# Two-token one-hots, groups built on a budget, and gate loads placed behind weight loads in a PEER layer

## The chip, the cores and the metric

The kernel runs on one core of one Trainium2 chip. The metric is the device time of one execution in microseconds. A core has five engines with instruction streams of their own: PE (TensorE, matrix multiplies; the loads of its stationary operand are listed as PEld), DVE (VectorE), ACT (ScalarE), POOL (GpSimd) and SP (SyncE, which here only issues DMAs). A wait on another engine or on a DMA stops everything that stands behind it in the same stream.

## The reference

Two layers of one transformer block and then two layers of a second block are applied to 256 tokens of width 1024, in float32. The change touches the feed-forward part of the second block alone, which chooses 128 of 16384 experts for each token (8 heads, 16 choices each):

```python
def peer_ffn(xn, wq, sub_keys, u_tab, v_tab):          # t = 256 tokens, d = 1024
    q = jnp.matmul(xt, wq).reshape(t, PEER_HEADS, 2, PEER_SUBDIM)
    scores = jnp.einsum('thcd,hcnd->thcn', q, sub_keys)
    sv, si = lax.top_k(scores, PEER_TOPK)              # 16 of 128, on either half
    cand_s = (sv[:, :, 0, :, None] + sv[:, :, 1, None, :]).reshape(t, PEER_HEADS, -1)
    cand_i = (si[:, :, 0, :, None] * 128 + si[:, :, 1, None, :]).reshape(t, PEER_HEADS, -1)
    best_s, best_p = lax.top_k(cand_s, PEER_TOPK)
    idx = jnp.take_along_axis(cand_i, best_p, axis=-1) # expert = 128 i + j
    gate = jax.nn.softmax(best_s, axis=-1)
    act = jnp.einsum('td,thkd->thk', xt, u_tab[idx])
    wgt = jax.nn.gelu(act) * gate
    return jnp.einsum('thk,thkd->td', wgt, v_tab[idx])
```

## The kernel before

`peer` does not gather rows of the tables. It computes the activations of all 16384 experts for all 256 tokens, multiplies them by a dense table of gates that is zero where an expert was not chosen, and multiplies the product by the whole table V. Each layer therefore streams both tables through the core in units of 128 x 1024 float32 (512 KB): 128 units of U, then 128 of V.

A unit is fetched by SP into `wx` (3 buffers; the next fetch is queued when a buffer is free), copied in reduced precision by ACT to `wh` and its remainder formed by DVE in `wl` (4 buffers each, lines 118 and 121 of `split`). PE then makes three products of every pair, high by high, high by low and low by high.

**U.** 64 steps in two halves of 32. A step (`u_step`) takes two units, runs 48 matmuls of 256 columns into the accumulator `pj`, and ACT applies Gelu from `pj` into `at0` (first half) or `at1` (second half). Meanwhile the first half carries the choice of the experts. Its gates reach the product in two ways. For tokens 0 to 127 POOL scatters them into a table in DRAM, `gates` (`scatter_gates`, which runs far into the second half). For tokens 128 to 255 they are built on the chip, four tokens at a time, in 32 groups: `build(g)` lets DVE form one-hots of the two halves of the expert number (`oi`, `oj`, 512 elements on each partition), multiply `oj` by the gate in three bf16 parts (`og`, 1536 elements), then PE multiplies them (12 matmuls of 128 x 128 into `ps`, three for each token), and DVE multiplies `at0` and the finished part of `at1` by `ps`; where `at1` is not yet computed ACT copies `ps` into it, and a later `u_step` multiplies its Gelu (in the tile `y`) onto that. Four tokens are interleaved, so that one token's one-hot has elements four apart:

```python
io = self.t(ip, [128, 128, 4], BF16, tag="io")
self.mm(ps[:, k], oi[:, :, k], og[:, n, :, k], k == 0 and n == 0, n == 2)
```

Before, one group is built behind each of the 32 steps of U's second half.

**V.** 64 steps. `v_split` loads two planes of the table for the tokens 0 to 127 (`gate`, 128 KB, 3 buffers), multiplies the activations by them on DVE (`at<-at,gate`), and splits the product into `eh` (ACT) and `el` (DVE). `v_step` runs 24 matmuls of 512 columns of its two units against it, accumulated in four banks (`big`). The split for step n+1 is issued in step n. A scheduler of the framework puts the instructions of each engine in an order by priorities and estimated times; loads that need no buffer yet in use may be queued early.

Of the kernel before, what the change touches and what calls it, by code (L numbers as in the profile page):

```python
# [12 lines left out]
BF16 = mybir.dt.bfloat16  # L13
# [3 lines left out]
AF = mybir.ActivationFunctionType  # L17
OP = mybir.AluOpType
AX = mybir.AxisListType

T = 256
# [32 lines left out]
EARLY = 1  # L54
WARM = 10
LAG, TAIL, AHEAD, HOLD = 4, 2, 2, (2, 6)
SIDE_Q, SIDE_S = 2500, 2800
UQ_SIZES = [768, 512]
S2_SIZES = [1024] * 26

# [1 line left out]
class Net:  # L62
# [83 lines left out]
    def weights(self, ap, sizes, per=1024, beside=iter(())):  # L146
        k, off = 0, 0
        while k < len(sizes):
            n, tot = 0, 0
            while k + n < len(sizes) and tot + sizes[k + n] <= per:  # L150
                tot += sizes[k + n]
                n += 1
            x = self.t(self.wp, [128, per], tag="wx", bufs=WX)
            self.nc.sync.dma_start(x[:, :tot], ap[:, off:off + tot])
            next(beside, None)
            at = 0
            for s in sizes[k:k + n]:
# [61 lines left out]

    def load_gates(self, l, n, pool):  # L220

        g = self.t(pool, [128, 2, 128], tag="gate", bufs=3)
        d = self.nc.sync.dma_start(g, self.gates[l][:, 2 * n:2 * n + 2]).ins
        for b in self.landed:
            self.tc.add_manual_dep(d, b.name, SYNC, reason="the gates have landed")
        return g
# [809 lines left out]
    def peer(self, l):  # L1036
# [3 lines left out]
        with ExitStack() as ctx:  # L1040
            ip = ctx.enter_context(self.pool("pi"))
            idx = self.t(ip, [128, 128], U32, tag="idx")
            gs = [self.t(ip, [128, 8, 16], tag=f"gs{tt}") for tt in range(2)]
# [13 lines left out]
            def u_step(at, jp, tb=0):  # L1057
# [4 lines left out]
                a = at[:, 2 * jp:2 * jp + 2]  # L1062
                self.act(a[:, :, :T - tb], ps[:, :, :T - tb], AF.Gelu_apprx_tanh)
# [5 lines left out]
            def build(g):  # L1069


                t0, done = 124 - 4 * g, 2 * g + 2
                oi, oj = (self.t(self.op, [128, 128, 4], BF16, tag=n, bufs=2) for n in ("oi", "oj"))
                og = self.t(self.op, [128, 3, 128, 4], BF16, tag="og", bufs=2)
                self.tt(oi, io, iT[:, None, t0:t0 + 4].to_broadcast([128, 128, 4]), OP.is_equal)
                self.tt(oj, io, jT[:, None, t0:t0 + 4].to_broadcast([128, 128, 4]), OP.is_equal)
                self.tt(og, oj[:, None].to_broadcast([128, 3, 128, 4]),
                        gT[:, :, None, t0:t0 + 4].to_broadcast([128, 3, 128, 4]), OP.mult)
                yield 1900
                ps = self.ps([128, 4, 128])  # L1080
                for k in range(4):
                    for n in range(3):
                        self.mm(ps[:, k], oi[:, :, k], og[:, n, :, k], k == 0 and n == 0, n == 2)
                ps = ps.rearrange("p t j -> p j t")
                t0 += 128
                a0, a1 = at0[:, :, t0:t0 + 4], at1[:, :, t0:t0 + 4]
                self.tt(a0, a0, ps[:, :64], OP.mult)
                self.tt(a1[:, :done], a1[:, :done], ps[:, 64:64 + done], OP.mult)
                if done < 64:
                    self.copy(a1[:, done:], ps[:, 64 + done:])  # L1090
                yield 700

            parts, loaded = {}, {}

            def g_load(n):
                if n < 64:
                    loaded[n] = self.load_gates(l, n, early)
# [11 lines left out]
            def first_split():  # L1109
                for n in range(2):  # L1110
                    g_load(n)
                v_split(0, early)

            def v_step(at, jp, half):
                units = [(next(w), x) for x in parts.pop(32 * half + jp)]
# [24 lines left out]
            with self.pool("pn") as npool:  # L1140
                lead = self.enter(npool, "add", self.v("n2"), w, self.t(npool, [128, 8, T], tag="xnew"))
                self.dump(f"xc{l}", self.xT)
                if l < DEPTH - 1:
                    nc.sync.dma_start(keep, self.xT)
                self.hctx.close()
                self.xctx.close()
                self.open_xs()
                pool = sctx.enter_context(self.pool("pk", "right"))
                self.token_column()
                if l == DEPTH - 1:  # L1150
                    nc.sync.dma_start(keep, self.rows_of(npool))
# [5 lines left out]
                self.copy(io, it[:, :, None].to_broadcast([128, 128, 4]))  # L1157
# [12 lines left out]
            self.hctx.close()  # L1170
            self.open_xt()
            if l < DEPTH - 1:
# [5 lines left out]
                end = to_output  # L1178
            vctx = ExitStack()
            vp = vctx.enter_context(self.pool("pv", "right"))  # L1180
            for half, at in enumerate((at0, at1)):
                weave(lambda jp: v_step(at, jp, half), iter(()), 0)
            vctx.close()
# [3 lines left out]
    def select(self, l, pool, w, lead, normed, io16, gs, idx, turned):  # L1187
# [63 lines left out]
        def rest_of_ranks():  # L1251
            yield from normed
            pend.sort(key=lambda x: x[0])
            for tt in range(2):
# [5 lines left out]
                for r in range(8):  # L1260
                    n = 16 if r == 0 else 8
                    o = 0 if r == 0 else 8 + 8 * r
# [5 lines left out]
                    yield 760  # L1268

                bt = best[tt]  # L1270
                g = gs[tt]
# [9 lines left out]
                pf = self.t(pool, [128, 128], tag="pf", bufs=2)  # L1281
# [37 lines left out]
                iT, jT, gT = turned  # L1319
                ps = self.ps([128, 3, 128])  # L1320
# [217 lines left out]
```

## Time and profile before

| | before |
|---|---|
| median of 3 runs | 2614.23 us (2613.8 to 2616.39) |
| profiled execution, and its span | 2614.9 us, 2613.0 us |
| granted TensorE clock | 0.996 of full speed |
| PE busy | 2560.8 us (98%) |
| PEld busy | 2366.2 us (91%) |
| DVE busy | 1835.9 us (70%) |
| ACT busy | 1383.7 us (53%) |
| POOL busy | 463.4 us (18%) |
| HBM | 179 GB/s over the span |

The span is what the trace covers; the execution's own time has 1.9 us around it. Busy time of PE is not time at its peak: matmuls are pipelined, and a matmul's listed duration is longer than the spacing of two in a row. In layer 1 U's second half runs from about 1046 to 1276 us and V to 1641 us; in layer 2 V begins at 2250 us and ends at 2608 us.

### The profile page before, as it was taken

What the parts mean: (1) busy time and instruction counts of PE and PEld (TensorE: products, weight loads), DVE (VectorE), ACT (ScalarE), POOL (GpSimd) and SP (SyncE); (2) the same over time, 40 slices, a digit from 0 to 9 for tenths busy, and PEclk for the clock granted to TensorE, in tenths of its full rate; (3) what the DMA queues carried; (4) which work ended last, traced back from release to release, by engine and by line L of the source; (5) the groups of instructions that cost most, each with busy time, mean ns of one, the idle gap of its engine ahead of it and who ended that gap; (6) DMA issues with size and microseconds to landing.
All of it is one profiled execution on the core that took longest, in us unless ns stands there. A gap on an engine that the chain in (4) does not pass through costs nothing.

```text
span 2613.0 us, 46153 instructions
## 1 busy us (share of the span) xinstructions
PE 2560.8 (98%) x18042; PEld 2366.2 (91%) x18042; DVE 1835.9 (70%) x3511; ACT 1383.7 (53%) x2128; POOL 463.4 (18%) x261
## 2 busy tenths in 40 slices
PE   8999999999999999999999999999999999999999
PEld 7799997999999999999878888999999999878887
DVE  6688777877887995666665555877994666675555
ACT  6565566655676554444444444776554443344443
POOL 0000000000000077773000000000178772000000
PEclk9999999999999999999999999999999999999999
DMA  8756652566535576665576666635576665676664
GB/s 281 235 179 192 183 174 79 153 192 183 175 116 185 170 185 186 149 150 149 193 249 203 194 194 193 185 107 187 173 191 179 148 150 148 212 248 194 194 194 158
DMA packets 195098, 470.95 MB, mean 180 GB/s; under 512 B 54644, under 2 KB 89588, under 8 KB 193856
## 3 DMA queue, kind: packets, MB, share of 16 engines
q1 hardware_dynamic: 158016, 467.86, 56.9%
q0 software_dynamic: 36864, 0.15, 3.6%
q8 instruction: 141, 2.31, 0.3%
q14 instruction: 77, 0.63, 0.1%
HBM read 447.86 MB, written 20.05 MB: 179 GB/s over the span
## 4 chain that ended last, share of the span: by engine, by line
PE 85%; DMA 6%; DVE 6%; ACT 2%; issue 1%; SPq 0%; ACTq 0%; DVEq 0%
PE pj L132 46%; PE big L132 31%; PE ps L132 7%; DMA gate<-gates 4%; DVE wl L121 2%; DMA wx<-in_w 1%; ACT wh L118 1%; PE ps L573 1%; DVE el L121 1%; DVE xn L124 0%; DVE at L121 0%; DVE xT L121 0%; DMA wx<-in_wq 0%; DVE xl L124 0%; DVE c L124 0%
## 5 line engine op out<-in xcount | busy, mean ns | idle before, releaser
L118 ACT ACTIVATE wh<-wx 128x1024 fp32r<-128x1024 f32 (+1 forms) x800 | 844.4, 1057 | 898.7 <-PE pj L132 356.1
L121 DVE TENSOR_TENSOR wl<-wx,wh 128x1024 fp32r<-128x1024 f32 (+1 forms) x800 | 975.0, 1220 | 453.8 <-ACT wh L118 446.4
L132 PE MATMUL pj<-xh,wh 128*128 128x256 f32 x3136 | 897.3, 286 | 10.5 <-ACT wh L118 7.9
L132 PE MATMUL pj<-xl,wh 128*128 128x256 f32 x3136 | 889.6, 284 | 3.3 <-DVE xl L124 2.7
L132 PE MATMUL pj<-xh,wl 128*128 128x256 f32 x3136 | 889.1, 284 | 3.8 <-DVE wl L121 3.8
L209 POOL DMA_INDIRECT gates<-gs,idx x256 | 462.9, 1808 | 1712.6 <-DVE idx L129 1591.8
L132 PEld LDWEIGHTS pj<-xh,wh 128*128 128x128 f32 x3136 | 601.2, 192 | 12.8 <-ACT wh L118 8.3
L132 PEld LDWEIGHTS pj<-xl,wh 128*128 128x128 f32 x3136 | 600.5, 191 | 7.9 <-DVE xl L124 6.5
L132 PEld LDWEIGHTS pj<-xh,wl 128*128 128x128 f32 x3136 | 599.9, 191 | 6.6 <-DVE wl L121 5.7
L132 PE MATMUL big<-wh,el 128*128 128x512 f32 x1024 | 402.1, 393 | 10.4 <-DVE el L121 10.3
L132 PE MATMUL big<-wh,eh 128*128 128x512 f32 x1024 | 400.0, 391 | 11.6 <-ACT eh L118 11.6
L132 PE MATMUL big<-wl,eh 128*128 128x512 f32 x1024 | 399.9, 390 | 0.0
L132 PEld LDWEIGHTS big<-wh,el 128*128 128x128 f32 x1024 | 193.1, 189 | 58.4 <-DVE el L121 19.2
L132 PEld LDWEIGHTS big<-wh,eh 128*128 128x128 f32 x1024 | 193.0, 189 | 52.6 <-ACT eh L118 12.2
L132 PEld LDWEIGHTS big<-wl,eh 128*128 128x128 f32 x1024 | 193.1, 189 | 39.6
L121 DVE TENSOR_TENSOR at<-at,ps 128x256 f32<-128x256 f32 (+20 forms) x128 | 45.1, 352 | 131.6 <-PE ps L132 131.6
L132 PE MATMUL ps<-og,oi 128*128 128x128 bf16 x768 | 101.5, 297 | 0.0
L132 PE MATMUL big<-gh,wh 128*128 128x256 f32 x352 | 99.1, 282 | 0.0
L132 PE MATMUL big<-gl,wh 128*128 128x256 f32 x352 | 98.9, 281 | 0.0
L132 PE MATMUL big<-gh,wl 128*128 128x256 f32 x352 | 98.8, 281 | 0.0
L121 DVE TENSOR_TENSOR at<-at,gate 128x256 f32<-128x256 f32 x128 | 52.9, 422 | 58.4 <-DMA gate<-gates 58.0
L121 DVE TENSOR_TENSOR el<-at,eh 128x512 fp32r<-128x512 f32 x128 | 87.2, 684 | 0.0
(355 smaller groups left out, 3309.0 us busy)
## 6 DMA issues: line engine op xcount, KB each, us to landing
wx<-in_u SPq DMA_DIRECT2D x256, 512.0 KB
wx<-in_v SPq DMA_DIRECT2D x256, 512.0 KB
wx<-in_wm SPq DMA_DIRECT2D x132, 512.0 KB
wx<-in_w SPq DMA_DIRECT2D x88, 512.0 KB
gates<-zero SPq DMA_DIRECT2D x128, 128.0 KB
wx<-in_wo SPq DMA_DIRECT2D x32, 512.0 KB
wx<-in_wq SPq DMA_DIRECT2D x32, 512.0 KB
gate<-gates SPq DMA_DIRECT2D x128, 128.0 KB
```

The lines of the kernel that those rows point to most:

```text
L118: return self.nc.scalar.activation(out, in_, AF.Copy)
L121: return self.nc.vector.tensor_tensor(out, a, b, op=op)
L132: return self.nc.tensor.matmul(ps, w, x, start=start, stop=stop, skip_group_check=True)
L209: d = self.nc.gpsimd.indirect_dma_start(flat, IndirectOffsetOnAxis(ap=idx[:, p:p + 1], axis=0), g[:, p:p + 1], None, compute_op=OP.add).ins
L573: self.nc.tensor.transpose(tp[:, kt, qt * 128:(qt + 1) * 128], p[:, qt, kt * 128:(kt + 1) * 128], self.ident)
```

## The change

It has four parts.

1. One-hots interleave two tokens instead of four (`io` is 128 x 2, `oi` and `oj` are 2 x 128 x 2). `oi` and `oj` stay one operation each; `og` becomes two operations of 768 elements. The 12 matmuls of a group stay, and read elements two apart.
2. The groups are a generator, `builds`, woven into U's second half on a budget: each of the 32 steps adds 3100, a group costs 2000 for its one-hots and matmuls and 750 for what uses `ps`. So a group's `ps` is used a step after it was started, now and then two groups fall into one step, and all are done some three steps before U's end. The tile `y` goes: Gelu is taken in place in `pj`, and DVE multiplies from there.
3. The first gates and V's first split (`first_split`) are issued in the last of U's steps, from a tile of their own; only steps 1 and 2 have their gates loaded at V's start.
4. `load_gates` makes each load of gates stand behind the latest unit's fetch in SP's queue (`self._dep(d, self.fetched)`).

```diff
-            x = self.t(self.wp, [128, per], tag="wx", bufs=WX)
-            self.nc.sync.dma_start(x[:, :tot], ap[:, off:off + tot])
+            self.fetched = self.nc.sync.dma_start(x[:, :tot], ap[:, off:off + tot]).ins
...
-        g = self.t(pool, [128, 2, 128], tag="gate", bufs=3)
+        g = pool if n == 0 else self.t(pool, [128, 2, 128], tag="gate", bufs=3)
         d = self.nc.sync.dma_start(g, self.gates[l][:, 2 * n:2 * n + 2]).ins
+        self._dep(d, self.fetched)
...
-            io = self.t(ip, [128, 128, 4], BF16, tag="io")
+            io = self.t(ip, [128, 128, 2], BF16, tag="io")
+            first = self.t(ip, [128, 2, 128], tag="gate")
+            built = [0]
...
-                if tb:
-                    y = self.t(self.op, [128, 2, 128], tag="y", bufs=2)[:, :, :tb]
-                    self.act(y, ps[:, :, T - tb:], AF.Gelu_apprx_tanh)
-                    self.tt(a[:, :, T - tb:], a[:, :, T - tb:], y, OP.mult)
+                if built[0]:
+                    self.act(ps[:, :, n:], ps[:, :, n:], AF.Gelu_apprx_tanh)
+                    self.tt(a[:, :, n:], a[:, :, n:], ps[:, :, n:], OP.mult)
...
+            def builds(pairs):
+                for t0 in range(124, -1, -4):
+                    oi, oj = (self.t(self.op, [128, 2, 128, 2], BF16, tag=n, bufs=b) for n, b in (("oi", 2), ("oj", 1)))
...
+                    ps = self.ps([128, 4, 128])
+                    for a in range(2):
+                        og = self.t(self.op, [128, 3, 128, 2], BF16, tag="og", bufs=3)
...
+                                self.mm(ps[:, 2 * a + k], oi[:, a, :, k], og[:, n, :, k], a == 0 and k == 0 and n == 0,
+                                        n == 2)
+                    yield 2000
...
+                    built[0] += 4
+                    yield 750
...
             def v_split(n, pool):
                 if n < 64:
-                    g_load(n + 2)
+                    if n:
+                        g_load(n + 2)
...
             with self.pool("po") as self.op:
-                for g in range(32):
-                    u_step(at1, g, 4 * g)
-                    for _ in build(g):
-                        pass
-            early = ctx.enter_context(self.pool("pf"))
-            first_split()
+                weave(u_second, builds(pairs), SIDE_G, first_split)
```

How the order of instructions moves is seen at three places. In the rows, `x<-y,z` is what is written and read, and the number is the tile's.

On DVE, in a step late in U's second half of layer 1, before:

```order
L121 TENSOR_TENSOR oj_15377<-io_9886,jT_9884 128x512
L121 TENSOR_TENSOR wl_15170<-wx_15166,wh_15169 128x1024
L121 TENSOR_TENSOR at_10626<-at_10626,ps_15119 128x64x4
L121 TENSOR_TENSOR wl_15227<-wx_15224,wh_15226 128x1024
L121 TENSOR_TENSOR at_13122<-at_13122,y_15110 128x2x88
L121 TENSOR_TENSOR at_13122<-at_13122,ps_15119 128x46x4
L121 TENSOR_TENSOR oi_15288<-io_9886,iT_9883 128x512
L121 TENSOR_TENSOR og_15290<-oj_15289,gT_9885 128x1536
L121 TENSOR_TENSOR oj_15464<-io_9886,jT_9884 128x512
```

And in the same place after the change:

```order
L121 TENSOR_TENSOR oi_15589<-io_9885,iT_9882 128x512
L121 TENSOR_TENSOR oj_15590<-io_9885,jT_9883 128x512
L121 TENSOR_TENSOR og_15594<-oj_15590,gT_9884 128x768
L121 TENSOR_TENSOR og_15602<-oj_15590,gT_9884 128x768
L121 TENSOR_TENSOR at_10626<-at_10626,ps_15505 128x64x4
L121 TENSOR_TENSOR at_13123<-at_13123,ps_15416 128x52x4
L121 TENSOR_TENSOR at_13123<-at_13123,pj_15433 128x2x112
L121 TENSOR_TENSOR wl_15614<-wx_15611,wh_15613 128x1024
L121 TENSOR_TENSOR wl_15645<-wx_15641,wh_15644 128x1024
```

Before, the products of `at0` and `at1` with `ps` (15119) stood around one `wl` and the product with `y`. After, they stand behind the next group's one-hots and both operations on `og`; the product of `at1` reads the `ps` of the group before (15416) the one that the product of `at0` reads (15505), and both `wl` of the step's units follow.

On SP, at the turn from U to V in layer 1 (`in_v` are V's units, `keep` the residual, `xT` its place in the memory that U's inputs leave), before:

```order
L154 DMA wx_16033<-in_v 128x1024
L1173 DMA xT_15941<-keep_9889 128x2048
L223 DMA gate_15926<-gates_95 128x256
L223 DMA gate_15928<-gates_95 128x256
L223 DMA gate_15930<-gates_95 128x256
L154 DMA wx_16039<-in_v 128x1024
L223 DMA gate_15970<-gates_95 128x256
L223 DMA gate_16014<-gates_95 128x256
L223 DMA gate_16057<-gates_95 128x256
L223 DMA gate_16101<-gates_95 128x256
L223 DMA gate_16144<-gates_95 128x256
L223 DMA gate_16188<-gates_95 128x256
```

And after:

```order
L154 DMA wx_16067<-in_v 128x1024
L1180 DMA xT_15971<-keep_9889 128x2048
L223 DMA gate_15976<-gates_95 128x256
L223 DMA gate_15978<-gates_95 128x256
L223 DMA gate_16004<-gates_95 128x256
L154 DMA wx_16073<-in_v 128x1024
L154 DMA wx_16110<-in_v 128x1024
L223 DMA gate_16048<-gates_95 128x256
L223 DMA gate_16091<-gates_95 128x256
L154 DMA wx_16116<-in_v 128x1024
L223 DMA gate_16135<-gates_95 128x256
L154 DMA wx_16154<-in_v 128x1024
```

Before, 64 loads of gates could run ahead of the fetches, eight and three between two of them. After, V's first gates (`gate_9886`, twelve rows up the queue) are loaded among U's last units, three more stand at the turn, and from there on one load of gates stands behind every second fetch, as in

```order
L154 DMA wx_16415<-in_v 128x1024
L154 DMA wx_16421<-in_v 128x1024
L223 DMA gate_16439<-gates_95 128x256
L154 DMA wx_16458<-in_v 128x1024
L154 DMA wx_16464<-in_v 128x1024
L223 DMA gate_16483<-gates_95 128x256
```

On DVE, at V's start in layer 1, before:

```order
L121 TENSOR_TENSOR at_10626<-at_10626,gate_15926 128x2x128
L121 TENSOR_TENSOR at_10626<-at_10626,gate_15928 128x2x128
L121 TENSOR_TENSOR at_10626<-at_10626,gate_15930 128x2x128
L121 TENSOR_TENSOR el_15934<-at_10626,eh_15933 128x512
L121 TENSOR_TENSOR el_15974<-at_10626,eh_15973 128x512
L121 TENSOR_TENSOR el_16018<-at_10626,eh_16017 128x512
L121 TENSOR_TENSOR at_10626<-at_10626,gate_15970 128x2x128
L121 TENSOR_TENSOR at_10626<-at_10626,gate_16014 128x2x128
L121 TENSOR_TENSOR at_10626<-at_10626,gate_16057 128x2x128
L121 TENSOR_TENSOR at_10626<-at_10626,gate_16101 128x2x128
L121 TENSOR_TENSOR at_10626<-at_10626,gate_16144 128x2x128
L121 TENSOR_TENSOR wl_15999<-wx_15995,wh_15998 128x1024
```

And after, where the first step's product and `el` were done in U, and 15976 is the gates of step 1:

```order
L121 TENSOR_TENSOR at_13123<-at_13123,pj_15901 128x2x128
L121 TENSOR_TENSOR wl_16033<-wx_16029,wh_16032 128x1024
L121 TENSOR_TENSOR wl_16070<-wx_16067,wh_16069 128x1024
L121 TENSOR_TENSOR at_10626<-at_10626,gate_15976 128x2x128
L121 TENSOR_TENSOR at_10626<-at_10626,gate_15978 128x2x128
L121 TENSOR_TENSOR at_10626<-at_10626,gate_16004 128x2x128
L121 TENSOR_TENSOR el_16008<-at_10626,eh_16007 128x512
L121 TENSOR_TENSOR el_16052<-at_10626,eh_16051 128x512
L121 TENSOR_TENSOR at_10626<-at_10626,gate_16048 128x2x128
L121 TENSOR_TENSOR at_10626<-at_10626,gate_16091 128x2x128
```

The product with the gates of step 1 now stands behind the remainders of four units of V, the last of them the sixth unit (16070). From there on the product for a step stands right before the remainder of the unit two behind the fetch that its load followed:

```order
L121 TENSOR_TENSOR at_10626<-at_10626,gate_16396 128x2x128
L121 TENSOR_TENSOR wl_16374<-wx_16371,wh_16373 128x1024
L121 TENSOR_TENSOR el_16356<-at_10626,eh_16355 128x512
L121 TENSOR_TENSOR wl_16381<-wx_16377,wh_16380 128x1024
L121 TENSOR_TENSOR at_10626<-at_10626,gate_16439 128x2x128
L121 TENSOR_TENSOR wl_16418<-wx_16415,wh_16417 128x1024
```

`gate_16439` was queued behind the fetch of 16421, whose buffer `wl_16374` sets free; its product stands one row before `wl_16418`, two units later.

## Rows read from the trace of the kernel before

**Rows 1.** Page: the last chain by engine and line, shares of the span.

```profile
PE pj L132 46%; PE big L132 31%; PE ps L132 7%; DMA gate<-gates 4%; DVE wl L121 2%; DMA wx<-in_w 1%; ACT wh L118 1%; PE ps L573 1%; DVE el L121 1%; DVE xn L124 0%; DVE at L121 0%; DVE xT L121 0%; DMA wx<-in_wq 0%; DVE xl L124 0%; DVE c L124 0%
```

**Rows 2.** Chain of waits, U's second half: start us, us, what.

```profile
1060.65 5.76 PE pj L132 x48
1067.84 5.76 PE pj L132 x48
```

**Rows 3.** Groups by shape, 1060 to 1260 us: busy us, mean ns, idle before.

```profile
L132 PE MATMUL ps<-og,oi 128*128 128x128 bf16 x330 | 43.7, 297 | 0.0
L132 PEld LDWEIGHTS <-oi 128*128 128x128 bf16 x328 | 35.0, 118 | 1.6
...
L121 DVE TENSOR_TENSOR wl<-wx,wh 128x1024 fp32r<-128x1024 f32 x56 | 68.5, 1223 | 8.7 <-ACT wh L118 8.1
...
L121 DVE TENSOR_TENSOR og<-oj,gT 128x1536 bf16<-128x1536 bf16 x28 | 26.6, 949 | 0.0
L121 DVE TENSOR_TENSOR at<-at,ps 128x256 f32<-128x256 f32 x28 | 11.8, 421 | 57.5 <-PE ps L132 57.5
L121 DVE TENSOR_TENSOR oi<-io,iT 128x512 bf16<-128x512 bf16 x28 | 11.7, 418 | 0.0
```

**Rows 4.** Whole run: PE and PEld groups by shape, one line of PE's timeline.

```profile
L132 PE MATMUL pj<-xl,wh 128*128 128x256 f32 x3136 | 889.6, 284 | 3.3 <-DVE xl L124 2.7
...
L132 PEld LDWEIGHTS ps<-vv,sz 128*128 128x128 f32 x72 | 8.5, 191 | 0.2
...
774.77 1.45 PE L132 MATMUL ps<-vv,sz 128*128 128x64 f32 x12
```

**Rows 5.** PE timeline, both starts and one end of V: start, us, idle.

```profile
1281.82 1.22 PE L132 MATMUL big<-wh,eh 128*128 128x512 f32 x2 [5.80 <-ACT eh L118]
...
1283.27 0.63 PE L132 MATMUL big<-wl,eh 128*128 128x512 f32 x1
...
1640.95 0.39 PE L132 MATMUL big<-wl,eh 128*128 128x512 f32 x1
...
2250.64 1.22 PE L132 MATMUL big<-wh,eh 128*128 128x512 f32 x2 [5.77 <-ACT eh L118]
```

**Rows 6.** Windows in V: busy us of engines, clock, DMA share, GB/s.

```profile
1300.00:1374.00 74.00, 68.38 (x291) 53.43 (x290) 52.63 (x84) 31.65 (x36) 0.00 (x0) 1.00 0.79 248
1374.00:1630.00 256.00, 256.00 (x1130) 212.03 (x1130) 144.98 (x144) 124.83 (x142) 0.00 (x0) 1.00 0.62 195
...
2250.60:2343.00 92.40, 87.54 (x364) 69.02 (x365) 64.76 (x106) 39.06 (x45) 0.00 (x0) 0.98 0.77 242
```

**Rows 7.** Chain of waits in V of layer 1: start us, us, what.

```profile
1275.14 5.52 DMA gate<-gates
...
1304.58 4.19 DMA gate<-gates
1311.32 3.80 DMA gate<-gates
...
1336.47 3.42 DMA gate<-gates
...
1373.81 265.28 PE big L132 x1169
```

**Rows 8.** Timelines of DVE, ACT and SP's queue from 1299.9 us.

```profile
1300.07 0.43 DVE L121 TENSOR_TENSOR at<-at,gate 128x256 f32<-128x256 f32 x1 [2.14 <-DMA gate<-gates]
1300.41 1.22 DVE L121 TENSOR_TENSOR wl<-wx,wh 128x1024 fp32r<-128x1024 f32 x1
...
1299.93 1.06 ACT L118 ACTIVATE wh<-wx 128x1024 fp32r<-128x1024 f32 x1 [1.66 <-PE big L132]
1300.90 0.61 ACT L118 ACTIVATE eh<-at 128x512 fp32r<-128x512 f32 x1
...
1301.66 0.33 SPq L154 DMA_DIRECT2D wx<-in_v  x1
1302.08 0.86 SPq L223 DMA_DIRECT2D gate<-gates  x2
```

More of the change, by code (lines that the diff above doesn't have):

```diff
@@ L56 @@
 LAG, TAIL, AHEAD, HOLD = 4, 2, 2, (2, 6)
-SIDE_Q, SIDE_S = 2500, 2800
+SIDE_Q, SIDE_S, SIDE_G = 2500, 2800, 3100
 UQ_SIZES = [768, 512]
@@ L1042, in peer @@
             idx = self.t(ip, [128, 128], U32, tag="idx")
-            gs = [self.t(ip, [128, 8, 16], tag=f"gs{tt}") for tt in range(2)]
+            gs = self.t(ip, [128, 8, 16], tag="gs")
             iT, jT = (self.t(ip, [128, 128], BF16, tag=n) for n in ("iT", "jT"))
             gT = self.t(ip, [128, 3, 128], BF16, tag="gT")
-            io = self.t(ip, [128, 128, 4], BF16, tag="io")
+            io = self.t(ip, [128, 128, 2], BF16, tag="io")
+            first = self.t(ip, [128, 2, 128], tag="gate")
+            built = [0]
             for _ in self.clear:
@@ L1055, in half_acts, with u_step @@
                 return self.t(ctx.enter_context(self.pool("pa")), [128, 64, T], tag="at")
-            def u_step(at, jp, tb=0):
+            def u_step(at, jp):
                 ps = self.pj([128, 2, T])
@@ L1061, in u_step @@
                     self.proj_fm(w, ps[:, m])
-                a = at[:, 2 * jp:2 * jp + 2]
-                self.act(a[:, :, :T - tb], ps[:, :, :T - tb], AF.Gelu_apprx_tanh)
-                if tb:
-                    y = self.t(self.op, [128, 2, 128], tag="y", bufs=2)[:, :, :tb]
-                    self.act(y, ps[:, :, T - tb:], AF.Gelu_apprx_tanh)
-                    self.tt(a[:, :, T - tb:], a[:, :, T - tb:], y, OP.mult)
[L1069 to L1091, printed above, removed]
@@ new lines, in u_step @@
+                a, n = at[:, 2 * jp:2 * jp + 2], T - built[0]
+                self.act(a[:, :, :n], ps[:, :, :n], AF.Gelu_apprx_tanh)
+                if built[0]:
[4 more added lines that the diff above has]
+                    oi, oj = (self.t(self.op, [128, 2, 128, 2], BF16, tag=n, bufs=b) for n, b in (("oi", 2), ("oj", 1)))
+                    chosen = lambda x: x[:, t0:t0 + 4].rearrange("p (a t) -> p a t", t=2)[:, :, None].to_broadcast([128, 2, 128, 2])
+                    for o, x in ((oi, iT), (oj, jT)):
+                        self.tt(o, io[:, None].to_broadcast([128, 2, 128, 2]), chosen(x), OP.is_equal)
+                    ps = self.ps([128, 4, 128])
+                    for a in range(2):
+                        og = self.t(self.op, [128, 3, 128, 2], BF16, tag="og", bufs=3)
+                        self.tt(og, oj[:, a:a + 1].to_broadcast([128, 3, 128, 2]),
+                                gT[:, :, None, t0 + 2 * a:t0 + 2 * a + 2].to_broadcast([128, 3, 128, 2]), OP.mult)
+                        for k in range(2):
+                            for n in range(3):
+                                self.mm(ps[:, 2 * a + k], oi[:, a, :, k], og[:, n, :, k], a == 0 and k == 0 and n == 0,
+                                        n == 2)
+                    yield 2000
+                    ps, done = ps.rearrange("p t j -> p j t"), 2 * pairs[0]
+                    a0, a1 = (x[:, :, 128 + t0:132 + t0] for x in (at0, at1))
+                    self.tt(a0, a0, ps[:, :64], OP.mult)
+                    self.tt(a1[:, :done], a1[:, :done], ps[:, 64:64 + done], OP.mult)
+                    if done < 64:
+                        self.copy(a1[:, done:], ps[:, 64 + done:])
+                    built[0] += 4
+                    yield 750
@@ L1096, in g_load @@
                 if n < 64:
-                    loaded[n] = self.load_gates(l, n, early)
+                    loaded[n] = self.load_gates(l, n, vp)
             def v_split(n, pool):
                 if n < 64:
-                    g_load(n + 2)
+                    if n:
+                        g_load(n + 2)
                     a = (at0, at1)[n // 32][:, 2 * (n % 32):2 * (n % 32) + 2]
@@ L1107, in v_split @@
                     parts[n] = [(h[:, m], low[:, m]) for m in range(2)]
[L1109 to L1112, printed above, removed]
             def v_step(at, jp, half):
@@ L1156, in peer @@
                 self.copy(io16, it[:, 0:16, None].to_broadcast([128, 16, 128]))
-                self.copy(io, it[:, :, None].to_broadcast([128, 128, 4]))
+                self.copy(io, it[:, :, None].to_broadcast([128, 128, 2]))
             self.xs = self.xh, self.xl
@@ L1162, in peer, with u_second, first_split @@
             at1 = half_acts()
-            with self.pool("po") as self.op:
-                for g in range(32):
-                    u_step(at1, g, 4 * g)
-                    for _ in build(g):
-                        pass
-            early = ctx.enter_context(self.pool("pf"))
-            first_split()
+            early = ctx.enter_context(self.pool("pf"))
+            pairs = [0]
+            def u_second(jp):
+                u_step(at1, jp)
+                pairs[0] += 1
+            def first_split():
+                loaded[0] = self.load_gates(l, 0, first)
+                v_split(0, early)
+            with self.pool("po") as self.op:
+                weave(u_second, builds(pairs), SIDE_G, first_split)
             self.hctx.close()
@@ L1180, in peer @@
             vp = vctx.enter_context(self.pool("pv", "right"))
+            for n in (1, 2):
+                g_load(n)
             for half, at in enumerate((at0, at1)):
@@ L1270, in rest_of_ranks @@
                 bt = best[tt]
-                g = gs[tt]
+                g = gs if tt == 0 else self.t(pool, [128, 8, 16], tag="g")
                 self.tt(g, bt, bt[:, :, 0:1].to_broadcast([128, 8, 16]), OP.subtract)
```

## The prediction

> **What bounds the kernel now.** The page comes first: its last chain is 46% `pj`, 31% `big` and 7% `ps`, all on PE [rows 1]. So most of the span is matmuls in a row, and a change pays where it makes matmuls cheaper or takes out a place where PE waits. The change touches two stages in each layer, and each is read by itself.
>
> *U's second half.* In the chain of waits one step's 48 matmuls take 5.76 us, and the next step begins 7.18 us later (1067.84 less 1060.65) [rows 2]. The 1.42 us between are the group's 12 small matmuls: 0.118 us each, against 5.76/48 = 0.120 for one of 256 columns, though they have 128 columns. The groups by shape say the same: a small bf16 one is listed with 297 ns, one of 256 columns with 284 [rows 3, 4]. So it passes at half the rate per column. What halves it? The load of its stationary operand takes 118 ns against 191 for float32, and with such 191 ns loads 12 matmuls of 64 columns pass in 1.45 us [rows 3, 4], so loads of 118 ns should allow 0.118/0.191 x 1.45/12 = 0.075 each. That leaves the moving operand `og`, read with elements four apart. DVE is not the bound here: it stands 57.5 us of these 200 us before `at<-at,ps`, waiting for PE [rows 3].
>
> *V.* At its start PE stands for 5.80 us (layer 2: 5.77) until `eh` of the first step is there [rows 5]; the chain names the loads of gates, issued when U ends, 5.52 us [rows 7]. After that gap some seven matmuls are listed with 0.63 instead of the 0.39 us of V's end [rows 5]: the slower of the clock's two levels. Then the chain consists of gate loads, one for each step, 13 pieces with 3.80 us in their middle and 4.19 and 3.42 to either side [rows 7], until at 1373.81 it turns to PE alone, 1169 matmuls in 265.28 us, 0.2269 each [rows 7]. The windows agree: PE is busy for 68.38 of 74 us before that and for 256 of 256 after; in layer 2 for 87.54 of 92.40 [rows 6]. At 0.2269 V's 1536 matmuls need 348.6 us. Layer 1 needs, from U's last matmul (1281.82 less 5.80) to V's (1640.95 + 0.23), 365.2: 16.6 lost. Layer 2 loses 5.8 in the gap and 92.40 - 364 x 0.2269 = 9.8 behind it, 15.6. Together 32.2 us: that is all the V part can give.
>
> **The change, part by part.**
>
> *Elements two apart.* 64 groups x 12 = 768 matmuls. The price of 128 columns at full rate is not in the trace. From below: 512 columns pass in 0.2269 and 256 in 0.120, so 128 on the same line are 0.0665. From above 0.118, if something else than the step holds them. The bound by loads, 0.075, lies near the lower end; I take 0.070. That saves 768 x 0.048 = 37 us (0 to 40). The Trainium skill, SBUF — State Buffer, in the property table at its head, says that a 16-byte line wants at least two hits for full bandwidth; eight bytes apart there are two hits already, so by it `og` was never slow and this part would give 0. The row of 297 ns speaks against that, but doesn't exclude it: rival B. For a stream of loads and matmuls of 128 columns the same notes (TensorE: Matmul & The Clock Gate, Back-to-back issue gap) give about 81 ns; by that the part would be 768 x 0.037 = 28 us. No run here shows it.
>
> *One-hots on DVE.* `og` in two operations: 512 elements take 0.418 and 1536 take 0.949 [rows 3], so 0.152 fixed and 0.519 for 1000 elements; 768 cost 0.55, two of them 0.15 more than before, 32 times a layer. A step's DVE work: two `wl` 2.45, `oi` and `oj` 0.84, `og` 1.10, products with `ps` and Gelu about 0.8 (`at<-at,ps` is 0.42 [rows 3], the other two grow and shrink against each other), 5.2 us, and a tenth of the group's part more where two groups share a step. PE's step becomes 5.76 + 0.84 = 6.6. So it stays hidden, under PE. The bound above: if pairs of four bytes drop DVE to the pace of a float32 operation (`wl`: 1024 in 1.22, so about 0.68 for 512), a step is 6.7 to 7.0 and DVE binds: rival D.
>
> *Budget, `y` away.* `ps` is used a step later, so no engine waits for it in the step; in place of `y` DVE reads `pj`, which frees that accumulator later than ACT did. There are two, so the next step has the other, and DVE has a whole step of PE's for it: 0. Where DVE falls behind by a step that cover is gone and PE waits, which is rival D. Groups end three steps before U does, so the last of U's steps are without them: no time of its own, the matmuls are only moved.
>
> *First split in U.* Its gates are queued among U's last units, and a load that waited for POOL there would hold the fetches behind it; POOL is through with its scatter long before, so I price that at 0. The gap of 5.8 us and the wait for `eh` go. But what is late next? On DVE the product with step 1's gates stands behind the remainder of V's sixth unit. With four `wh` and `wl`, that one needs the buffer of unit 1, free when PE is through step 0: 24 x 0.2269 = 5.45 us after U's end. Then come `wh` 1.06, `wl` 1.22, the product 0.34 to 0.43, `eh` 0.61 [rows 8]: 3.3 us in which PE has nothing. The gates themselves, queued behind `xT<-keep` as before, land 5.5 us after U's end and the product would be theirs then: not binding. So 5.8 becomes 3.3. If the clock drops again after it, as the seven or so matmuls at 0.63 instead of 0.39 show it did before, up to 7 x 0.24 = 1.7 is lost (0 to 1.7): I take 0.8.
>
> *Loads behind fetches.* The crowd of loads at V's start goes, but each load now stands in a loop: `wl` frees a buffer, the fetch is issued and 0.42 us later the load (1301.66 to 1302.08), the gates land after g, the product takes 0.34 (1300.07 to 1300.41), and the remainder two units on 1.22, which frees the next [rows 8]. That is g + 1.98, or about g + 2.05 with the semaphores, for one step, and a step has 5.45. It binds where g exceeds 3.4. Above, 13 loads of the crowded stretch: 3.80 in the middle. That stretch had DMA at 0.79 and 248 GB/s; a step after the change moves 1.125 MiB in 5.45 us, 216 GB/s, between it and the 195 of V's rest [rows 6]. So g should be under 3.8, and I take 3.55, between the middle piece and the 3.42: 0.15 us over in each of 64 steps is 9.6. DVE has a lead to eat first: with four buffers `wl` may be three units ahead, 3 x 2.72 less the 1.06 and 1.22 that a unit takes, 5.9 us. So 3.5 stay. Below, g under 3.4: 0. Above, g = 4.2, as the piece of 4.19: rival C.
>
> *Sum.* V after: 348.6 + 3.3 + 0.8 + 3.5 = 356.2 a layer, 7.6 lost; 2 x 7.6 = 15.2 against 32.2 is -17.0. With -37, 2614.9 becomes 2561. The median shown is 0.7 below the profiled execution: 2560.
>
> **Rivals.**
> A, as above. Its own range is 2545 to 2575 (small matmuls at 0.0665 to 0.081, V losing 0 to 12 a layer).
> A+, V with hardly any loss (g under 3.4, no drop of the clock) and the matmuls at 0.0665: -40 and -25, so 2549, and 2542 if the small ones come lower still.
> B, the small matmuls stay at 0.118: the load of `oi`, whose 118 ns are just that spacing, or the switch from one group to the next sets them. For it speaks that coincidence; against it the 64-column row. Only V gains: 2597. The Trainium skill's rule of two hits on a line (SBUF — State Buffer) would end here as well.
> C, the other side: the loop of gates binds all of V. At g = 4.2 a step is 6.25, 64 x 0.80 - 5.9 + 4.1 = 49.4 lost a layer against 16.1: +67, and with -37 the time is 2645. It turns slower than before where 64(g - 3.40) exceeds 16.1 + 18.5 + 1.8, at g about 3.97. For it speaks that half of the 13 pieces lie at 3.8 or above [rows 7]; against it, that there were two to four loads in a step.
> C/2, g of 3.7 to 3.85: 64 x 0.30 to 0.45 less 1.8, so 17 to 27 lost a layer, +3 to +22 in V: 2581 to 2600.
> D, DVE binds U: 29 steps at 7.0 instead of 6.6 take 12 a layer back: 2585.
>
> **How the numbers follow.** Chances: A 0.45, A+ 0.08, B 0.14, C 0.10, C/2 0.15, D 0.08. A is the forecast, 2560. The range must reach from A+ to C/2 and B: 2542 to 2606, leaving out C and the ends. What a measurement of this kernel can tell from no change is about 0.2%, 5 us; only a g between 3.9 and 4.0, or B with some of C, falls there: 0.05. C above it and B together with C/2 make slower 0.11. Faster is the rest, 0.84.
>
> **What would show it.** In the chain a step of U's second half: 6.6 us apart while groups run, 5.76 at the end, and the small ones listed well below 297 ns. Between U and V no gap, then one of about 3.3 us at 5.4 us into V, released by ACT's `eh` or DVE's `el`. In V, PE busy for all but a few us; a chain made of `gate` pieces all through V would be C, with their length its g. `at<-at,ps` without a wait for PE. The prediction is wrong if the small ones keep their spacing, if DVE shows no idle time in U's second half, or if loads of gates need over 3.9 us.

## The result

The changed kernel takes 2568.62 us (median of 4 runs, 2567.0 to 2571.33), the kernel before 2614.02 beside it (4 runs): a ratio of 0.9828, 95% interval 0.9811 to 0.9845, 45 us less. The forecast was 2560, with 2542 to 2606 as its range and 2545 to 2575 for its case A. The profiled execution has a span of 2565.2 us against 2613.0; 4 us of that difference lie ahead of the places that were changed (the chain's piece of 528 matmuls in U's first half begins at 984.70 us instead of 988.71), and are no part of the change. The page's chain by line now reads so, against [rows 1]:

```profile
PE pj L132 48%; PE big L132 24%; DMA gate<-gates 9%; PE ps L132 6%; DVE wl L121 4%; SPq L154 1%; ACT wh L118 1%; PE ps L574 1%; DVE xn L124 1%; DVE xT L121 0%; DVE xl L124 0%; DMA wx<-in_w 0%; DVE c L124 0%; DMA sel<-in_sel 0%; DMA wx<-in_wm 0%
```

The share of gate loads did not go, it rose from 4% to 9%, and with it `wl` and SP. That is the first sign that the two halves of the forecast fared differently.

**U's second half.** The chain of waits, to be held against [rows 2]. The first row is one group, the rows at 1088.56 and 1095.87 enclose a doubled group, and the last row is the end of U, four steps without a group:

```profile
1055.35 0.70 PE ps L132 x12
...
1062.56 5.80 PE pj L132 x48
1069.06 5.80 PE pj L132 x48
...
1088.56 5.80 PE pj L132 x48
1095.87 5.80 PE pj L132 x48
...
1227.51 22.97 PE pj L132 x191
```

A step with a group takes 6.50 us instead of 7.18, one with two groups 7.31, one without a group 5.76 (191 matmuls in 22.97). With 24, 4 and 4 steps of 6.50, 7.31 and 5.76 the half takes 208.3 us; 32 steps of 7.18 took 229.8. That is 21.5 us in each layer, 43 in all. The groups by shape from 1060 to 1240 us answer to [rows 3]; the row of the load of `oi` is that of the whole run:

```profile
L121 DVE TENSOR_TENSOR wl<-wx,wh 128x1024 fp32r<-128x1024 f32 x55 | 67.2, 1222 | 39.9 <-ACT wh L118 39.3 <-issue 0.6
L121 DVE TENSOR_TENSOR og<-oj,gT 128x768 bf16<-128x768 bf16 x56 | 29.0, 554 | 3.9 <-PE ps L132 3.1
L132 PE MATMUL ps<-og,oi 128*128 128x128 bf16 x348 | 24.8, 219 | 0.0
...
L121 DVE TENSOR_TENSOR at<-at,ps 128x256 f32<-128x256 f32 x29 | 12.0, 414 | 1.0 <-PE ps L132 1.0
...
L121 DVE TENSOR_TENSOR oi<-io,iT 128x512 bf16<-128x512 bf16 x28 | 11.7, 418 | 0.0
...
L132 PEld LDWEIGHTS <-oi 128*128 128x128 bf16 x768 | 44.3, 97 | 3.1
```

A small matmul is listed with 219 ns instead of 297, `og` with 554 (0.55 was worked out), `oi` as before with 418, so interleaving two tokens costs DVE nothing there, and `at<-at,ps` waits 1.0 us instead of 57.5. DVE still stands 40 us before `wl`: it does not bind.

**V.** The timeline of PE at V's start and end in layer 1, and the window over its whole length (the columns are those of [rows 6]):

```profile
1250.43 0.40 PE L132 MATMUL big<-wh,eh 128*128 128x512 f32 x1
...
1259.23 1.19 PE L132 MATMUL big<-wh,eh 128*128 128x512 f32 x4 [3.18 <-ACT eh L118]
...
1614.08 0.39 PE L132 MATMUL big<-wl,eh 128*128 128x512 f32 x1
```

```profile
1250.40:1614.30 363.90, 358.54 (x1546) 285.63 (x1545) 211.98 (x256) 172.21 (x198) 0.00 (x0) 1.00 0.66 211
```

V follows U without a gap, and the wait of 3.3 us foretold for step 1 is there with 3.18. But V takes 363.9 us, 15.3 over its 348.6, where the kernel before took 365.2. Layer 2 is alike (2196.79 to 2560.96, 364.2). Of the 17 us foretold, V gave about 1. Where the rest went is in the chain of waits of V:

```profile
1333.55 1.23 DVE wl L121
1334.77 0.02 issue
1334.79 0.33 SPq L154
1335.12 0.05 issue
1335.17 3.68 DMA gate<-gates
1338.84 0.02 issue
1338.87 0.06 DVE at L121
...
1339.21 1.23 DVE wl L121
```

Read downward it is the loop that the prediction described: `wl` frees a buffer, SP issues the fetch and then the load of gates, the load lands after 3.68 us, DVE takes the product, and the next `wl` follows. From one `wl` to the next of the kind are 5.66 us, two units on, where PE needs 5.45. The loop does not reach PE in the first steps, while DVE's lead lasts (the chain is PE alone for 68.33 us from 1259.23); then it binds to V's end with breaks. DVE shows the same from its side, a wait for gates in every step, while PE hardly has a wait: it is busy for 358.54 of 363.90 us, and its matmuls come a little further apart. The rows of DVE:

```profile
1338.87 0.43 DVE L121 TENSOR_TENSOR at<-at,gate 128x256 f32<-128x256 f32 x1 [2.37 <-DMA gate<-gates]
1339.21 1.22 DVE L121 TENSOR_TENSOR wl<-wx,wh 128x1024 fp32r<-128x1024 f32 x1
1340.35 0.68 DVE L121 TENSOR_TENSOR el<-at,eh 128x512 fp32r<-128x512 f32 x1
1340.95 1.22 DVE L121 TENSOR_TENSOR wl<-wx,wh 128x1024 fp32r<-128x1024 f32 x1
1344.58 0.43 DVE L121 TENSOR_TENSOR at<-at,gate 128x256 f32<-128x256 f32 x1 [2.42 <-DMA gate<-gates]
```

### The profile page after: what moved, and what is told of

Its sections match the earlier page's. It is cut to its first block, busy times and chain, and to the rows that moved or that the text cites. A ratio compares the mean times of both kernels' runs of the same rounds, so it can differ in the third digit from the quotient of the medians.

```text
span 2565.2 us, 46088 instructions
## 1 busy us (share of the span) xinstructions
PE 2525.6 (98%) x18042; PEld 2316.3 (90%) x18042; DVE 1828.1 (71%) x3575; ACT 1389.3 (54%) x2130; POOL 483.9 (19%) x261
## 4 chain that ended last, share of the span: by engine, by line
PE 80%; DMA 10%; DVE 7%; ACT 2%; issue 1%; SPq 1%; DVEq 0%; ACTq 0%
PE pj L132 48%; PE big L132 24%; DMA gate<-gates 9%; PE ps L132 6%; DVE wl L121 4%; SPq L154 1%; ACT wh L118 1%; PE ps L574 1%; DVE xn L124 1%; DVE xT L121 0%; DVE xl L124 0%; DMA wx<-in_w 0%; DVE c L124 0%; DMA sel<-in_sel 0%; DMA wx<-in_wm 0%
## 5 line engine op out<-in xcount | busy, mean ns | idle before, releaser
L209 POOL DMA_INDIRECT gates<-gs,idx x256 | 483.3, 1888 | 1673.9 <-DVE idx L129 1553.4
L132 PE MATMUL big<-wh,el 128*128 128x512 f32 x1024 | 408.6, 399 | 4.2 <-DVE el L121 3.5
L118 ACT ACTIVATE eh<-at 128x512 fp32r<-128x512 f32 x128 | 78.4, 614 | 3.3 <-DVE at L121 3.3
L124 DVE SCALAR_TENSOR_TENSOR c<-lz,v,c 128x255 f32<-128x255 f32 x176 | 73.7, 477 | 0.9 <-ACT c L111 0.8
```

The lines of the kernel that those rows point to most:

```text
L118: return self.nc.scalar.activation(out, in_, AF.Copy)
L124: return self.nc.vector.scalar_tensor_tensor(out, a, s, b, op0=op0, op1=op1)
L132: return self.nc.tensor.matmul(ps, w, x, start=start, stop=stop, skip_group_check=True)
L209: d = self.nc.gpsimd.indirect_dma_start(flat, IndirectOffsetOnAxis(ap=idx[:, p:p + 1], axis=0), g[:, p:p + 1], None, compute_op=OP.add).ins
```

## The experiments

The theory after the result has two parts. In U, the whole gain is the step between the elements of the moving operand `og`. In V, the gap and the crowd of loads were traded for a loop of about the same price, and the loop comes from the order on DVE, where a product stands only two units behind the unit that let its load start. The rivals: the budget and the later use of `ps` made U faster; it is the load of the stationary operand; V is bound by its traffic, or by loads issued too late.

### Which operand, and whether the stride alone

The kernel before with two tokens interleaved, and nothing else changed:

```diff
-            io = self.t(ip, [128, 128, 4], BF16, tag="io")
+            io = self.t(ip, [128, 128, 2], BF16, tag="io")
...
-                oi, oj = (self.t(self.op, [128, 128, 4], BF16, tag=n, bufs=2) for n in ("oi", "oj"))
-                og = self.t(self.op, [128, 3, 128, 4], BF16, tag="og", bufs=2)
+                oi, oj = (self.t(self.op, [128, 2, 128, 2], BF16, tag=n, bufs=2) for n in ("oi", "oj"))
+                og = [self.t(self.op, [128, 3, 128, 2], BF16, tag="og", bufs=4) for _ in range(2)]
...
-                        self.mm(ps[:, k], oi[:, :, k], og[:, n, :, k], k == 0 and n == 0, n == 2)
+                        self.mm(ps[:, k], oi[:, k // 2, :, k % 2], og[k // 2][:, n, :, k % 2], k == 0 and n == 0, n == 2)
```

> The kernel before, with one-hots of two tokens interleaved (og in two operations) and nothing else changed: one group behind each step, gates and first split as before. My theory: the gain in U is the step of the moving operand alone. Then U's second half takes 32 steps of about 6.5 us instead of 7.18, 21 to 22 us less in each layer, V stays as before: 2571 us. Rival: the gain came from using ps a step later and from building groups on a budget; then nothing moves: 2614 us.

2571.45 us, ratio to before 0.9829 (0.9813 to 0.9845): the same as the whole change. The chain of waits:

```profile
1054.35 5.80 PE pj L132 x48
1060.85 5.80 PE pj L132 x48
```

Steps of 6.50 us, although `ps` is used in its own step. V starts after a gap again (5.80 us in the kernel before):

```profile
1256.04 1.22 PE L132 MATMUL big<-wh,eh 128*128 128x512 f32 x2 [6.69 <-ACT eh L118]
```

So parts 2 to 4 of the change come to nothing in sum, as far as an interval of 4 us to either side can tell.

The changed kernel with four tokens again (in `builds`, tiles of 128 x 4, `og` in three operations):

```diff
-                    for a in range(2):
-                        og = self.t(self.op, [128, 3, 128, 2], BF16, tag="og", bufs=3)
...
+                    og = [self.t(self.op, [128, 128, 4], BF16, tag="og", bufs=4) for _ in range(3)]
...
+                            self.mm(ps[:, k], oi[:, :, k], og[n][:, :, k], k == 0 and n == 0, n == 2)
```

> The changed kernel with four tokens interleaved again (og in three operations of 512, one for each part of the gate); budget, first split in U and the place of the gate loads are kept. Theory (step of the moving operand alone): the small matmuls are back at 0.118 us, U's second half 22 us longer in each layer: 2612 us. Rival (ps a step later, budget): 2569 us.

2620.16 us, ratio 1.0014 (1.0004 to 1.0024), the theory's side and some us over it: V takes 368.5 and 371.3 us in the two layers of this run instead of 363.9 and 364.2, and why is not shown. A group is back at 1.43 us in the chain, and a step at 7.18:

```profile
1057.00 1.43 PE ps L132 x12
1058.42 5.75 PE pj L132 x48
1064.18 1.43 PE ps L132 x12
```

Then the two operands apart. First `oj` and `og` at two, `oi` at four:

```diff
+            io2 = self.t(ip, [128, 128, 2], BF16, tag="io2")
...
+                oi = self.t(self.op, [128, 128, 4], BF16, tag="oi", bufs=2)
+                oj = self.t(self.op, [128, 2, 128, 2], BF16, tag="oj", bufs=1)
```

> The kernel before with oj and og interleaving two tokens, while oi (the stationary operand) stays at four; a second iota table is added, groups stand as before. Theory (the moving operand's step sets the pace): the small matmuls come 0.057 to 0.060 us apart as with both at two, U's second half 208 us: about 2571 us. Rival (the stationary operand's load, 118 ns with elements four apart, sets it): 0.118 us apart, U's second half 230 us, 2615 us. Both in part: 0.07 to 0.08, that is, the load at about two thirds of its length.

2570.23 us in one run (before 2613.0 beside it). And the opposite, `oi` at two, `oj` and `og` at four:

> The opposite: oi interleaves two tokens, oj and og four; else the kernel before. Theory (moving operand): 0.118 us apart, U's second half 230 us, 2615 us. Rival (stationary operand's load): 0.057 to 0.060 us, 208 us, 2571 us.

2612.82 us in one run (the same 2613.0 beside it). The groups of the small matmuls and of their loads, whole run, the first kernel:

```profile
L132 PE MATMUL ps<-og,oi 128*128 128x128 bf16 x768 | 57.5, 223 | 0.0
L132 PEld LDWEIGHTS <-oi 128*128 128x128 bf16 x768 | 47.2, 115 | 2.8
```

and the second:

```profile
L132 PE MATMUL ps<-og,oi 128*128 128x128 bf16 x768 | 99.9, 295 | 0.0
L132 PEld LDWEIGHTS <-oi 128*128 128x128 bf16 x768 | 81.2, 114 | 3.0
```

The loads last the same in both, the matmuls do not. The pace is the moving operand's, and the load at four elements apart hides under it even at the faster pace. The listed length of a load does not follow its own step either: with `oi` at two it is 114 ns here and 97 in the changed kernel.

### What binds V

The changed kernel with the loads one step earlier and a buffer more:

```diff
-        g = pool if n == 0 else self.t(pool, [128, 2, 128], tag="gate", bufs=3)
+        g = pool if n == 0 else self.t(pool, [128, 2, 128], tag="gate", bufs=4)
...
-                        g_load(n + 2)
+                        g_load(n + 3)
...
-            for n in (1, 2):
+            for n in (1, 2, 3):
```

> The changed kernel with each load of gates issued one step earlier and four gate buffers instead of three. Theory: V is bound by a loop of order, since each product with gates stands on DVE two units of weights behind the unit whose buffer let the fetch and the load start; issued earlier, the product is placed a step earlier too, and the loop of load 3.7 us plus 2.0 us stays: 2568 us, same as the changed kernel. Rival: the loads are simply issued too late for the step that needs them; then a step more of lead hides them and V loses only the 3.2 us at its start: 2568 less 2 x 11 = 2546 us.

2576.05 us, ratio 0.9847 (0.9831 to 0.9864): no gain over the changed kernel's 0.9828 (0.9811 to 0.9845). The order shows why: the product that the earlier load allows is placed a step earlier too, still two units behind (`gate_16267`, queued behind the fetch of 16249, stands one row before `wl_16246`). The loop in its chain of waits is as before:

```profile
1401.85 3.86 DMA gate<-gates
...
1405.74 0.06 DVE at L121
...
1406.08 1.23 DVE wl L121
...
1407.32 0.33 SPq L154
```

Next, the loads left where they are, and the product of step n held behind the remainder of unit 2n-2 (`lows` keeps the last remainders):

```diff
-                    self.tt(a[:, :, :128], a[:, :, :128], loaded.pop(n), OP.mult)
+                    p = self.tt(a[:, :, :128], a[:, :, :128], loaded.pop(n), OP.mult)
+                    if n > 1:
+                        self._dep(p.ins, self.lows[-3])
```

> The changed kernel with the product with the gates of step n held behind the remainder of unit 2n-2 on DVE, nothing else (the loads stand in the queue as in the changed kernel). A product then stands six units behind the unit that let its load start instead of two. Theory (loop of order): the loop has 16 us for 5.7 and no longer binds, V's steps take 5.45 us, what stays is the 3.2 us wait at step 1: 2568.6 less 2 x 11 to 12 = 2546 us. Rival (V is bound by the traffic of fetches and loads itself, 1.125 MiB a step): no change, 2569 us. Rival (el is late when the product is late): slower than the changed kernel.

2545.57 us, ratio 0.9729 (0.9713 to 0.9745): 26 us under the changed kernel by the ratios, as the theory has it. The chain of V is PE from the first wait to the end, 1506 matmuls at 0.228 each, with the wait before it still there in PE's timeline:

```profile
1258.19 343.32 PE big L132 x1506
```

```profile
1258.19 1.22 PE L132 MATMUL big<-wh,eh 128*128 128x512 f32 x4 [3.18 <-ACT eh L118]
```

More bytes a second pass in it than in the changed kernel, 217 GB/s against 211 in layer 1's V, so the traffic was not the bound.

Then that wait as well: gates and product of step 1 among U's last steps (`og` gives a buffer for the room).

```diff
-                        og = self.t(self.op, [128, 3, 128, 2], BF16, tag="og", bufs=3)
+                        og = self.t(self.op, [128, 3, 128, 2], BF16, tag="og", bufs=2)
...
-                loaded[0] = self.load_gates(l, 0, first)
+                for n in (0, 1):
+                    loaded[n] = self.load_gates(l, n, first[:, 2 * n:2 * n + 2])
                 v_split(0, early)
+                a = at0[:, 2:4, :128]
+                self.tt(a, a, loaded.pop(1), OP.mult)
```

> The run with the late product, and in addition the product of step 1 is taken in U: the gates of steps 0 and 1 are loaded among U's last units, og has two buffers instead of three to make room, and only the first product at V's start (step 2) stands behind the sixth unit's remainder. Theory (PE's wait of 3.2 us at step 1 comes from the order on DVE, where the product stands behind a remainder whose buffer PE frees at the end of step 0): the wait goes in both layers, 6 to 8 us less than with the late product alone, a ratio to before of about 0.970, V at 349 to 351 us. Rival (the wait moves to another step, or U slows with fewer og buffers): no gain over the late product alone, ratio 0.973.

2535.91 us (5 runs), ratio 0.9703 (0.969 to 0.9716): the fastest kernel of the study, 33 us under the changed one by the ratios. V in the two layers is PE throughout, 349.1 and 348.4 us with an ideal of 348.6:

```profile
1249.30:1598.40 349.10, 349.10 (x1547) 289.08 (x1546) 216.05 (x255) 171.97 (x198) 0.00 (x0) 1.00 0.70 220
2179.80:2528.20 348.40, 348.38 (x1538) 288.14 (x1536) 214.38 (x254) 165.91 (x190) 0.00 (x0) 1.00 0.69 214
```

### The other parts of the change, one at a time

The first split written after U, as before (the tile `first` goes, and the gates of steps 0 to 2 are loaded there too):

```diff
+                for n in range(2):
+                    g_load(n)
...
-                weave(u_second, builds(pairs), SIDE_G, first_split)
+                weave(u_second, builds(pairs), SIDE_G)
+            early = ctx.enter_context(self.pool("pf"))
+            first_split()
```

> The changed kernel with the first split of V taken after U as before (its gates are loaded there too); two-token one-hots, budget and the place of the loads are kept. Theory (first split buys the gap of 5.8 us and the clock behind it, and pays 3.2 us at step 1): PE stands about 5.8 us at V's start again, the loop of gate loads costs the same 12 us a layer as in the changed kernel, 4 us more in each layer: ratio 0.986. Rival (the gap gives the loop its lead, and nothing is lost): ratio 0.983, same as the changed kernel.

2567.82 us, ratio 0.9821 (0.9806 to 0.9836). My expectation failed, and the rival's number came for another reason: there is no gap. With the groups done early and the loads behind the latest fetch, the scheduler takes the first split among U's steps anyway, though it is written after them. DVE's timeline, with U still running until 1250.6:

```profile
1242.10 0.69 DVE L121 TENSOR_TENSOR el<-at,eh 128x512 fp32r<-128x512 f32 x1
1242.70 0.42 DVE L121 TENSOR_TENSOR at<-at,gate 128x256 f32<-128x256 f32 x1
...
1246.57 0.43 DVE L121 TENSOR_TENSOR at<-at,gate 128x256 f32<-128x256 f32 x1 [2.27 <-DMA gate<-gates]
...
1252.35 0.43 DVE L121 TENSOR_TENSOR at<-at,gate 128x256 f32<-128x256 f32 x1 [2.28 <-DMA gate<-gates]
```

It has no wait of 3.18 us at step 1 either, and is not faster: the loop has started in U, 5.78 us from one of the waiting products to the next, and V takes 365.2 us in layer 1 (1250.55 to 1615.70) against 363.9. Where the loop binds, what PE gains at V's start is taken back by it. So this run does not show what the first split is worth with the gap in its place; no run of the changed kernel has the old gap.

One group behind each step, none doubled:

```diff
-SIDE_Q, SIDE_S, SIDE_G = 2500, 2800, 3100
+SIDE_Q, SIDE_S, SIDE_G = 2500, 2800, 2750
```

> The changed kernel with a budget of 2750 instead of 3100, just what a group costs: one group falls behind each of U's 32 steps and none is doubled, so the last group ends with U, and the first split of V comes after U's last step. Theory (the budget itself costs and saves nothing, as the 384 small matmuls of a layer are the same; it only makes room for the first split before U's end): U's second half as long as in the changed kernel, a gap of 2 to 6 us at V's start: ratio 0.983 to 0.987. Rival (doubled groups cost PE or DVE something): faster than the changed kernel.

2570.6 us, ratio 0.9834 (0.9819 to 0.9849), within the theory's bounds; the gap at V's start is 1.53 us, a little shorter than foretold. Against the changed kernel the difference cannot be told from none.

The loads of gates without their place behind the fetches:

```diff
-        self._dep(d, self.fetched)
```

> The changed kernel without the line that holds a load of gates behind the latest fetch. By the order of instructions the load of step 0 then stands on SP ahead of U's unit 51 of 128, and it must wait for POOL's last scatter, which ended at 1212 us in the changed kernel, while PE would use up the units fetched before it at about 1005 us. Theory (SP's stream waits with the load, and every later fetch behind it): PE stands some 200 us in each layer, 2950 to 3000 us. Rival (the load waits in the DMA queue only, or the fetches pass it): no such stand, and V as in the kernel before, about 2570 us.

2926.21 us in one run, a little less than worked out, since the scatter ended earlier (its last piece starts at 1171.10). The timelines of SP, ACT and PE:

```profile
1174.20 0.33 SPq L223 DMA_DIRECT2D gate<-gates  x1
```

```profile
1178.45 1.06 ACT L118 ACTIVATE wh<-wx 128x1024 fp32r<-128x1024 f32 x1 [185.29 <-DMA wx<-in_u]
```

```profile
1180.05 0.58 PE L132 MATMUL pj<-xh,wh 128*128 128x256 f32 x1 [179.28 <-ACT at L111]
```

SP's stream stands with the load until POOL's last scatter, no weights are fetched, ACT waits 185 us for them, and PE 179 us for ACT; the list of waits has two such, 357.8 us. Its V is the old one, with the crowd of loads: PE is busy for 353.73 of 363 us in layer 1, where the changed kernel's V takes 363.9. So the place in the queue buys nothing in V, but it is what makes an early first load possible.

## Why the prediction was right, and where it was off

The forecast of 2560 was 8 or 9 us too low, its range held, and the mechanisms were the ones named. That the time lies inside the range of case A is in part luck: V lost 15.3 and 15.6 us a layer, more than the 12 at which A's range ends, and U gave 6 us more than was taken. (By its own bounds that range is 2542 to 2578, not 2545 to 2575.)

**Elements two apart: right, the size a little small.** 37 us were taken, 43 measured. A small matmul costs (6.50 - 5.76)/12 = 0.062 us of a step (the chain's piece of twelve is 0.70, 0.058 each, and the 48 matmuls behind it take 5.80 instead of 5.76), less than the 0.070 taken and less than the lower end of 0.0665, which a straight line through 256 and 512 columns had given. Rival B (0.118 stays) is out, and the swap of the operands shows that it is `og` and not the load of `oi`. Elements eight bytes apart pass at 0.118 us a matmul, four bytes apart at 0.062; no run has them side by side. The Trainium skill's rule that was weighed there (SBUF — State Buffer, Specifications (TRN2)) asks for at least two hits on a 16-byte line for full bandwidth. By that rule eight bytes apart should have been free, and the measurement says otherwise.

**DVE, budget, `y`: right.** `og` takes 0.55, `at<-at,ps` waits 1.0 us for PE in all, DVE has 40 us idle before `wl`, and one group for each step costs the same. Rival D is out.

**First split: the mechanism right, its worth wrong.** The gap went, and 3.18 us at step 1 took its place, as worked out; behind it the granted clock stayed at 1.00 in layer 1 and was 0.93 from 2196.7 to 2221 us in layer 2, where some seven matmuls are listed with 0.63, so 0.8 was about the mean of the two. But the terms were added to that of the loop, and they do not simply add: in the run with the first split written after U the 3.18 us are gone and V is no shorter, while with the product held back, where the loop no longer binds, taking them out did pay.

**Loads behind fetches: the term that was mis-sized.** The prediction took g = 3.55 from pieces of a crowded stretch, argued that a thinner queue would be quicker, credited DVE with a lead of 5.9 us and left 3.5 us a layer (9.6 less 5.9 is 3.7). The 61 pieces in the chains of the two layers measure 3.44 to 4.00, 3.67 on average. The loop is g + 2.0 as foretold: 5.66 us on average over the 26 rounds from 1329.28 to 1476.45, a good 0.2 over PE's 5.45. The lead was too large as well. These are rows of DVE in layer 1:

```profile
1271.20 0.43 DVE L121 TENSOR_TENSOR at<-at,gate 128x256 f32<-128x256 f32 x1 [1.37 <-DMA gate<-gates]
...
1327.32 0.42 DVE L121 TENSOR_TENSOR at<-at,gate 128x256 f32<-128x256 f32 x1 [2.29 <-DMA gate<-gates]
...
1504.37 0.42 DVE L121 TENSOR_TENSOR at<-at,gate 128x256 f32<-128x256 f32 x1 [4.05 <-DMA gate<-gates]
```

The product waits for its gates in every step from 1271.20 on. The ten rounds to 1327.32, where the loop reaches PE, take 56.1 us and ten of PE's steps 54.5, so the lead was worth under 2 us. Once in each layer, besides, a load outside the chain took 5.4 us (queued at 1498.99, its product at 1504.37), and PE waited 1.6 us behind it. As an estimate, 0.22 in some 60 rounds is 13, less the lead and with the long load about 12.5; 15.3 less the first wait of 3.2 is 12.1. V lost 15.3 and 15.6 us a layer instead of 7.6: together 16 us more, less the 6 by which U did better, is about the miss. The 3.42 came from a stretch in which several loads hung on one fetch; behind a fetch of its own a load has 512 KB ahead of it each time. That this is what makes it 3.67 was not tested by itself, and what made the one load so long is not known. It is C/2 in mechanism and just under its edge (17 to 27 lost a layer), while A's time was nearer.

**Rival C.** The sign that the prediction gave for it, a chain of `gate` pieces through V, did come, with breaks. But to be slower than before it wanted a g of about 4 in every step, and only single loads come to it.

## What to carry to other kernels

Where a bf16 matmul of few columns passes no faster than one of twice the columns, look for a step between the elements of its moving operand and repack that first; here the stationary operand's step made no difference. When a wait is removed from a stage that streams, write down the loop that sets its pace next (buffer, fetch, load, product, buffer) with the number of units it spans: here a loop 4% over its budget cost 12 us over 64 steps, twice the gap of 5.8 us that was removed. A load issued earlier does not help if its consumer moves with it; holding the consumer back, behind the instructions that feed the queue, did.

## What was not expected of the hardware

Twelve matmuls of 128 columns with four-byte steps pass at 0.062 us each, faster than the line through longer ones had it, while their loads are listed with 97 to 115 ns: loads listed longer than the spacing of the matmuls still hide. And `oi` costs DVE 418 ns whether two tokens are interleaved or four.
